# Masks added on VectorE, row factors spread through DRAM, and a new order of pieces in a two-layer trunk

## The chip, the core and the metric

The kernel runs on one core of one Trainium2 chip. TensorE multiplies matrices into eight PSUM banks; VectorE, ScalarE (ACT in the profile) and GpSimd (POOL) do elementwise work; SyncE (SP) and, in places, GpSimd and ScalarE issue the transfers between DRAM and SBUF. The metric is the device time of one execution in microseconds; less is better.

## The reference

Everything is float32. x and mem are 256 rows of 1024, the model has two layers and a last RMS norm:

```python
for layer in range(2):
    h = rms_norm(x, norm_g[layer])
    proj = einsum('btd,dc->btc', h, w_in[layer])          # 1024 x 3584
    sb_q, sb_k, sb_v, sb_g, mb_q, mb_k, mb_v, mb_g, mem_q, mem_g = split(proj)
    o_sb  = stick_breaking_attention(sb_q, sb_k, sb_v) * silu(sb_g)      # 6 heads of 64
    o_mb  = moba_attention(rotary(mb_q), rotary(mb_k), mb_v) * silu(mb_g)  # 6 heads
    m = rms_norm(mem, mem_norm_g[layer])
    mk, mv = split(m @ w_mem_kv[layer])                   # 1024 x 512
    o_mem = memory_attention(mem_q, mk, mv) * silu(mem_g)  # 4 heads
    x = x + concat[o_sb, o_mb, o_mem] @ w_out[layer]      # 1024 x 1024
return rms_norm(x, final_norm_g)
```

Stick-breaking attention is strictly causal: a weight is sigmoid(z) times the product of 1 - sigmoid(z) over the later past positions, computed with logarithms and running sums. With 256 rows and blocks of 256, MoBA is a causal softmax over one block. So both kinds need a triangular mask of -1e30 on the scores of the 128 x 128 blocks on the diagonal, strict for the first, with the diagonal kept for the second. Memory attention has no mask.

## The kernel before

**Precision.** Every weight and every activation that enters a large product is kept as two parts: hi, the value in TensorE's fp32r type, and lo, what is left. A product is three matmuls: hi by hi, hi by lo, lo by hi. The parts of the weights are made on the chip: a cast writes hi (ScalarE or VectorE), a subtraction raw - hi writes lo (VectorE).

**Weights and chunks.** The weights are cut into pieces by group (sb_q, mb_k, ..., wo0 to wo2 for the output projection; the table `ORDER` says in which order each layer takes them), and each piece into chunks of 768 columns by 128 rows, 384 KB. Chunks pass through a ring of 5 raw buffers (`raw`) and 7 pairs hi/lo (`hl`). A raw buffer is loaded again, by SP, right behind the subtraction that read it last. So TensorE needs cast and subtraction of a chunk before it can use it, and VectorE's subtraction also releases the next transfer. A piece is either of the T kind (output transposed, columns on partitions: `hl` is the stationary side; the profile names the moving side first, so its rows read `bank<-T,hl`) or of the N kind (rows on partitions, `bank<-hl,T`). T is the normed activation's transpose in hi and lo.

**The norm of layer 0.** x^T is loaded as 8 row blocks of 128 x 256 into `uT` and scaled by the gains only (`T<-uT,gc`). The factor of each row of x (1/rms) is not known by then: x itself is loaded later (`xs`), its squares are summed on ScalarE, and the factor is multiplied in when a piece leaves PSUM. A piece of the N kind has its rows on partitions and takes the factor as a scalar per partition (`rcx`, `rcm` for mem). A piece of the T kind needs the factors along the free axis, the same on all partitions (`rbx`, `rbm`). For these, `row_stats` (L552 to L575) puts the factors on a diagonal (`dg`, hi and lo, VectorE), multiplies it by a matrix of minus ones on TensorE (`bank<-dg,negone`, float32r, two matmuls for each row block), and copies the result out with the sign turned. In layer 1 the rows are normed before they are transposed, and no factors are needed.

**Scores.** `pair_scores` (L651 to L684) does two heads at a time, in halves of the array (64 of the 128 rows). Behind the products of a pair it adds the mask by 4 bfloat16 matmuls of a mask with the identity, 128 x 128 each, for stick-breaking and MoBA alike. `sb_head` (L686) then has ScalarE read the scores; `soft_head` (L727) takes the maximum of each row with a `TENSOR_REDUCE` (L733) and ScalarE the exponential. The weights of MoBA and of memory attention are transposed in blocks of 32 x 32 on VectorE and turned the rest of the way by a trip through DRAM (`D` to `Z` and back), as are the rotated queries and keys.

**What sets the order.** Nothing is decided while the kernel runs. A planner in the program (class `Sched`) gives every engine its queue: tasks are generators that name the engine they want next and what they need; the planner keeps a clock for each engine from a table of costs, takes the task that can start first, and among those within a slack the one with the smaller priority. Priorities of score, sum and evacuation tasks stand where they are spawned; `_by_form` holds back the half-array products until there are `CROWD` of them, and its table of costs charges for each change between full and half array. Costs, lags, priorities and the loads' places (`X67_AT`, `CST_AT`, `X0_AT`) are constants at the head of the file.

**The start.** Two chunks are issued on ScalarE's queue and the rest on SP's, x^T blocks between them:

```python
load_xT(2, 3); dma_chunk(); load_xT(3, 4); load_xT(4, 6)     # L456 to L459
if j == X67_AT: load_xT(6, 8, now=now)                       # in dma_chunk, L409
```

In the rows, L243 is every matmul (helper `mm`), L259 and L261 ScalarE's copies and activations, L265, L269, L273 and L280 VectorE's forms (tensor by tensor, with scalar, scaling, copy), L346 every transfer of SP, L462 GpSimd's broadcast of a row.

Of the kernel before, what the change touches and what calls it, by code (L numbers as in the profile page):

```python
# [7 lines left out]
F32 = mybir.dt.float32  # L8
# [9 lines left out]
KT = 8  # L18
# [16 lines left out]
P_RX = 1
P_M0 = 12
P_RM = 12
P_M1 = 4
# [168 lines left out]
def hybrid_trunk(ctx: ExitStack, tc: tile.TileContext, x, mem, norm_g, w_in, w_mem_kv, w_out,  # L207
# [26 lines left out]
    def mm(out, lhsT, rhs, start, stop, **kw):  # L234
        n = _free(rhs)
        half = lhsT.shape[0] == 64 or out.shape[0] == 64
        if lhsT.dtype == FR:
            c = max(60.0, n * 0.4167 + 13.0)
# [4 lines left out]
        nc.tensor.matmul(out, lhsT=lhsT, rhs=rhs, start=start, stop=stop, **kw)  # L243
        m = (lhsT.shape[0], out.shape[0])
        S.op("pe", (0.5 * c if half else c) + pe_mode(m, lhsT.dtype))
# [48 lines left out]
    identb = sb("identb", [128, 128], BF)  # L294
    masks = sb("masks", [128, 2, 128], BF)
# [104 lines left out]
    def dma_chunk(now=0.0, q=None):  # L400
# [8 lines left out]
        if j == X67_AT:  # L409
            load_xT(6, 8, now=now)  # L410
# [48 lines left out]
    load_xT(4, 6)  # L459
# [5 lines left out]
    def setup():  # L465
        yield R("pool")
        nc.gpsimd.memset(negone.bitcast(F32), -1.0)
        S.op("pool", 2400.0)
# [3 lines left out]
        nc.gpsimd.tensor_copy(identb, ident)  # L472
        nc.gpsimd.tensor_copy(masks, m.rearrange("p (m c) -> p m c", m=2))
# [78 lines left out]
    def row_stats(l, t, src, key, rc, rb):  # L552
# [667 lines left out]
```

## Time and profile before

| quantity | value |
|---|---|
| time, median of 3 runs | 277.53 us (277.35 to 277.68) |
| the profiled execution | 277.43 us |
| its span | 275.7 us |
| TensorE busy | 268.5 us, 97%, 1709 matmuls |
| VectorE busy | 233.5 us, 85%, 524 instructions |
| ScalarE busy | 182.2 us, 66%, 408 instructions |
| GpSimd busy | 3.8 us, 10 instructions |
| moved by transfers | 62.08 MB, mean 225 GB/s |
| TensorE's granted clock | 0.9 and more in all slices but the last (0.8) |

The profile was taken in one execution; the span is the time between its first and its last record, the rest up to the execution's time lies before and behind. A group in the list of instructions has busy time, mean ns of one, then the idle time of its engine just before, and what ended it. In a piece of timeline, or of the chain of work that ended last, the columns are start, length and what ran; neighbouring instructions of one form stand in one row with their count. The ends of pipelined matmuls are modelled, so that of two rows one behind the other the difference of starts tells the pace, not the length.

### The profile page before, as it was taken

How to read it: one execution, taken by the hardware profiler on the slowest of the kernel's cores; microseconds unless marked ns; L12 is line 12 of the kernel's file. 1: busy time of each engine (PE TensorE's matmuls, PEld its weight loads, DVE VectorE, ACT ScalarE, POOL GpSimd, SP SyncE). 2: the span in 40 equal slices, each digit the busy share in tenths (PEclk: the TensorE clock that was granted, in tenths of full speed). 3: DMA queues.
4: the chain of work that ended last, by engine and by line, in shares of the span. 5: the costliest groups of instructions: out<-in, count | busy, mean ns of one | idle time of the engine just before them, and what ended most of it. 6: DMA issues, size and time to landing. Idle time of an engine off the chain costs nothing.

```text
span 275.7 us, 5015 instructions
## 1 busy us (share of the span) xinstructions
PE 268.5 (97%) x1709; PEld 241.4 (88%) x1709; DVE 233.5 (85%) x524; ACT 182.2 (66%) x408; POOL 3.8 (1%) x10
## 2 busy tenths in 40 slices
PE   8999999999999999999999999999999999999992
PEld 5879999889897898999988899988888898989991
DVE  4879999997999989996889588979889999886172
ACT  3788889995588385873885374549379799543053
POOL 0030000000000000000000000000000000000000
PEclk9999999999999999999999999999999999999998
DMA  6999975778749999873485865795768888580004
GB/s 219 355 394 352 374 249 194 215 218 278 248 134 304 308 289 305 237 256 119 155 267 170 269 185 187 273 300 172 235 216 237 268 214 219 162 269 10 0 0 152
DMA packets 47497, 62.08 MB, mean 225 GB/s; under 512 B 3696, under 2 KB 44016, under 8 KB 47472
## 3 DMA queue, kind: packets, MB, share of 16 engines
q1 hardware_dynamic: 46608, 59.93, 68.7%
q0 software_dynamic: 288, 1.05, 1.1%
q10 hardware_dynamic: 576, 0.79, 0.8%
q8 instruction: 13, 0.21, 0.3%
q14 instruction: 12, 0.10, 0.1%
HBM read 54.67 MB, written 7.08 MB: 224 GB/s over the span
## 4 chain that ended last, share of the span: by engine, by line
PE 93%; DMA 4%; ACT 1%; DVE 1%; SPq 0%; issue 0%; DVEq 0%
PE bank L243 92%; DMA raw<-in_w_in_dram 2%; DMA uT<-xT_dram 1%; PE bank L248 1%; DVE hl L265 0%; ACT hl L259 0%; SPq L346 0%; ACT T L261 0%; ACT ss L261 0%; DVE T L269 0%; ACT junk L261 0%; DVE hl L280 0%; DVE xs L273 0%; DVEq L1216 0%
## 5 line engine op out<-in xcount | busy, mean ns | idle before, releaser
L265 DVE TENSOR_TENSOR hl<-raw,hl 128x768 fp32r<-128x768 f32 (+2 forms) x112 | 101.4, 912 | 11.4 <-ACT hl L259 10.7
L243 PE MATMUL bank<-T,hl 128*128 128x512 f32 (+1 forms) x582 | 106.2, 339 | 0.5 <-DVE hl L265 0.5
L243 PEld LDWEIGHTS bank<-T,hl 128*128 128x128 f32 x582 | 88.9, 189 | 13.8 <-DVE hl L265 0.8
L259 ACT CAST hl<-raw 128x768 fp32r<-128x768 f32 (+2 forms) x99 | 79.0, 811 | 21.1 <-PE bank L243 12.6
L243 PE MATMUL bank<-hl,T 128*128 128x384 f32 (+1 forms) x448 | 81.8, 337 | 0.0
L243 PEld LDWEIGHTS bank<-hl,T 128*128 128x128 f32 x448 | 76.5, 188 | 1.9 <-issue 0.3
L243 PE MATMUL bank<-hl,mxhi 128*128 128x384 f32 (+1 forms) x192 | 45.0, 319 | 0.0
L243 PEld LDWEIGHTS bank<-hl,mxhi 128*128 128x128 f32 x192 | 33.3, 189 | 0.6 <-issue 0.6
L243 PE MATMUL bank<-hl,mxlo 128*128 128x384 f32 (+1 forms) x96 | 30.7, 319 | 0.0
L261 ACT ACTIVATE w<-bank,st 128x256 f32<-128x256 f32 (+1 forms) x40 | 17.3, 451 | 9.0 <-DVE st L733 9.0
L243 PEld LDWEIGHTS bank<-hl,mxlo 128*128 128x128 f32 x96 | 18.1, 189 | 0.5 <-DVE mxlo L265 0.4
L259 ACT COPY gT<-bank 128x256 f32<-128x256 f32 x16 | 5.9, 372 | 18.5 <-PE bank L243 18.3
L261 ACT ACTIVATE junk<-xs 128x384 bf16<-128x384 f32 (+2 forms) x15 | 8.0, 532 | 14.9 <-DVE xs L265 14.2
L261 ACT ACTIVATE ga<-ga 128x768 f32<-128x768 f32 (+1 forms) x24 | 15.1, 631 | 0.7 <-DVE ga L269 0.5
L733 DVE TENSOR_REDUCE st<-bank 128x1 f32<-128x256 f32 (+1 forms) x40 | 12.8, 372 | 1.6 <-PE bank L243 1.6
L261 ACT ACTIVATE T<-uT,gc 128x256 fp32r<-128x256 f32 x24 | 11.4, 502 | 3.6 <-DMA uT<-xT_dram 3.6
L265 DVE TENSOR_TENSOR xs<-bank,xs 128x384 f32<-128x384 f32 (+1 forms) x11 | 5.7, 519 | 8.9 <-PE bank L243 8.9
L763 DVE STREAM_TRANSPOSE D<-w 128x384 f32<-128x384 f32 (+1 forms) x20 | 12.4, 622 | 0.0
L269 DVE SCALAR_TENSOR_TENSOR T<-uT,gc,T 128x256 fp32r<-128x256 f32 x24 | 11.0, 478 | 1.0 <-ACT T L261 1.0
L261 ACT ACTIVATE a<-a 128x384 f32<-128x384 f32 x24 | 11.6, 527 | 0.1
L273 DVE TENSOR_SCALAR w<-w,st 128x256 f32<-128x256 f32 (+1 forms) x40 | 11.1, 327 | 0.0
L265 DVE TENSOR_TENSOR gT<-bank,gT 128x256 f32<-128x256 f32 x16 | 6.7, 419 | 4.3 <-ACT gT L259 3.9
(115 smaller groups left out, 250.1 us busy)
## 6 DMA issues: line engine op xcount, KB each, us to landing
raw<-in_w_in_dram SPq DMA_DIRECT2D x70, 384.0 KB, 4.6
raw<-in_w_out_dram SPq DMA_DIRECT2D x20, 384.0 KB, 4.5
Z<-D SPq DMA_DIRECT2D x10, 384.0 KB, 4.9
raw<-in_w_mem_kv_dram SPq DMA_DIRECT2D x8, 384.0 KB, 3.1
T<-Z SPq DMA_DIRECT2D x24, 96.0 KB, 4.6
uT<-memT_dram SPq DMA_DIRECT2D x8, 256.0 KB, 4.9
Z<-D SPq DMA_DIRECT2D x4, 512.0 KB, 4.3
T<-Z SPq DMA_DIRECT2D x24, 64.0 KB, 3.5
```

The source lines that it names most:

```text
L243: nc.tensor.matmul(out, lhsT=lhsT, rhs=rhs, start=start, stop=stop, **kw)
L248: nc.tensor.transpose(out, in_, idt)
L259: nc.scalar.copy(out, in_)
L261: nc.scalar.activation(out, in_, func, **kw)
L265: nc.vector.tensor_tensor(out, a, b, op=op)
L269: nc.vector.scalar_tensor_tensor(out, a, s, b, op0=op0, op1=op1)
L273: nc.vector.tensor_scalar(out, a, s, None, op0=op)
L733: nc.vector.tensor_reduce(st[:, t:t + 1], sc[:, r0:r1], axis=AX.X, op=OP.max, negate=True)
L763: nc.vector.transpose(o, w[:, :n * 128].rearrange("p (m j r) -> p m j r", j=4, r=32))
```

## The change

1. **Masks.** The matmuls with masks go. A stick-breaking head begins with one VectorE add in place, in PSUM, of a float32 mask to the two diagonal blocks of its scores. For a MoBA head, VectorE's `tensor_tensor_reduce` reads the scores and a mask, writes the negated masked scores to SBUF and keeps their minimum, in place of the `TENSOR_REDUCE`; ScalarE takes the exponential from SBUF with the sign turned, and the score bank is free before that. The mask tiles (`smask`, `cmask`) are float32.
2. **Row factors.** The diagonals and their matmuls go. The factors of 256 rows stand in two columns of a 128 x 32 tile, which VectorE transposes in 32 x 32 blocks (`rt`); GpSimd's queue dumps the 8 rows of 32 to DRAM (two transfers) and, behind them, spreads the row of 256 over all partitions (one transfer). Pieces of the N kind wait for their row block's factors alone and no longer for both.
3. **Start.** x^T blocks 4 to 7 are loaded one at a time, each behind one chunk, and x and the constants one or two chunks later.
4. **Order.** A new `ORDER` of pieces, new orders of the rows within wo pieces (`KORD`), gates computed as 2 + 1 blocks in place of 3 at once, `HALVES` empty (the trips' loads are no longer split in two), new priorities, costs and slacks of the planner.

```diff
-KORD = (0, 1, 2, 3, 4, 5, 6, 7)
+KORD = ((4, 5, 2, 3, 0, 1, 6, 7), (4, 5, 0, 1, 2, 3, 6, 7))
...
-X67_AT = 5
-CST_AT = 9
-X0_AT = 8
-X1_AT = 14
+X_AT = {5: 4, 6: 5, 7: 6, 8: 7}
+CST_AT = 11
+X0_AT = 9
+X1_AT = 15
...
-ORDER = (["sb_qk", "mb_k", "mb_q", "mb_g", "mk", "mv", "mem_q", "sb_v", "sb_g", "mb_v", "mem_g"],
-         ["mk", "mv", "mb_g", "mb_q", "mb_k", "mem_q", "sb_k", "sb_g", "sb_q", "mem_g", "sb_v", "mb_v"])
-GATES = {"sb_g": ((0, 1, 2),), "mb_g": ((0, 1, 2),), "mem_g": ((0,), (1,))}
+ORDER = (["sb_qk", "mb_q", "mb_k", "mk", "mem_q", "mv", "sb_g", "sb_v", "mb_g", "mb_v", "mem_g"],
+         ["mk", "mv", "mb_q", "mb_k", "sb_k", "sb_g", "mem_q", "sb_q", "sb_v", "mb_g", "mb_v", "mem_g"])
+GATES = {"sb_g": ((0, 1), (2,)), "mb_g": ((0, 1), (2,)), "mem_g": ((0,), (1,))}
...
-        if j == X67_AT:
-            load_xT(6, 8, now=now)
+        if j in X_AT:
+            load_xT(X_AT[j], X_AT[j] + 1, now=now)
...
-    load_xT(4, 6)
...
+        nc.gpsimd.tensor_scalar(smask, m[:, 128:256], -1.0, -1.0e30, op0=OP.is_ge, op1=OP.mult)
+        nc.gpsimd.tensor_copy(cmask[:, 128:256], m[:, 128:256])
...
-        yield R("dve", need=["cst"])
-        ts(dg[:, 0, :], ident, rc[:, t:t + 1])
-        yield R("dve")
-        stt(dg[:, 1, :], ident, rc[:, t:t + 1], dg[:, 0, :].bitcast(F32), OP.mult, OP.subtract)
-        _, (pt,) = yield R("pe", alloc=["bank"], need=["setup0"], late=DG_LATE)
-        mm(pt[:, :128], negone, dg[:, 0, :], True, False)
-        mm(pt[:, :128], negone, dg[:, 1, :], False, True)
-        yield R("dve")
-        ts(rb[:, t * 128:(t + 1) * 128], pt[:, :128], -1.0)
...
+    def rows_done(key, name, rb):
+        z = dpool.tile([1, 256], F32, name="rows_" + key)
+        yield R("dve", need=["setup0", (key, "rows", 0), (key, "rows", 1)])
+        nc.vector.transpose(rt, rcx if key == "x" else rcm)
+        S.op("dve", 100.0)
+        yield R("pool")
+        for t in range(2):
+            nc.gpsimd.dma_start(z[:, t * 128:t * 128 + 128].rearrange("o (i a) -> (o i) a", i=4), rt[t:128:32, :])
...
+        yield R("pool", need=[(name, "dump")])
+        nc.gpsimd.dma_start(rb, z.broadcast_to([128, 256]))
...
-        if kind != "mem":
-            yield R("pe")
-            for h in range(2):
-                for j, o in enumerate((slice(0, 128), slice(256, 384))):
-                    if kind == "sb":
-                        mm(sc[h][:, o], masks[:, 0, :], identb, False, j == 1)
-                    else:
-                        mm(sc[h][:, o], identb, masks[:, 1, :], False, j == 1)
...
-        _, (a,) = yield R("act", alloc=["a"], need=[("qkdone", l, "sb", h)])
+        yield R("dve", need=[("qkdone", l, "sb", h)])
         zb = scs.pop((l, "sb", h))
         z = zb[:, :384]
+        zd = zb.rearrange("p (j c) -> p j c", c=256)[:, :, 0:128]
+        tt(zd, zd, smask.unsqueeze(1).broadcast_to([128, 2, 128]), OP.add)
+        _, (a,) = yield R("act", alloc=["a"])
...
+                nc.vector.tensor_tensor_reduce(w[:, r0:r1], sc[:, r0:r1], cmask[:, 256 - r1 + r0:256], -1.0, 3.0e38,
+                                               OP.add, OP.min, st[:, t:t + 1])
...
+            S.free("bank", sc)
+            yield R("act")
+            for t, (r0, r1) in enumerate(reg):
+                act(w[:, r0:r1], w[:, r0:r1], AF.Exp, scale=-1.0, bias=st[:, t:t + 1], accum_out=st[:, 2 + t:3 + t])
```

Three places show what the new order moves. The first is SP's queue at the start: transfers of x^T blocks (`uT`) and weight chunks (`raw`, with the ring's buffer number). Before:

```order
L346 DMA uT_73<-xT_dram 128x256
L346 DMA raw4_93<-in_w_in_dram 128x768
L346 DMA uT_73<-xT_dram 128x256
L346 DMA uT_73<-xT_dram 128x2x256
L346 DMA raw0_89<-in_w_in_dram 128x768
L346 DMA uT_73<-xT_dram 128x2x256
L346 DMA raw1_90<-in_w_in_dram 128x768
```

And now:

```order
L352 DMA uT_73<-xT_dram 128x256
L352 DMA raw4_93<-in_w_in_dram 128x768
L352 DMA uT_73<-xT_dram 128x256
L352 DMA raw0_89<-in_w_in_dram 128x768
L352 DMA uT_73<-xT_dram 128x256
L352 DMA raw1_90<-in_w_in_dram 128x768
L352 DMA uT_73<-xT_dram 128x256
```

The pair of blocks ahead of the chunk in raw0 is gone, the pair behind it is one block, and the others follow behind later chunks.

The second is TensorE's queue at the end of the stick-breaking scores of layer 0, the last products of the third pair of heads and what stands behind (`bank` is a PSUM bank, `T0` the normed x or mem). Before:

```order
L243 MATMUL bank0_101<-sb_q_78,sb_k_80 128x256
L243 MATMUL bank1_102<-sb_q_78,sb_k_80 128x256
L243 MATMUL bank0_101<-sb_q_78,sb_k_80 128x128
L243 MATMUL bank1_102<-sb_q_78,sb_k_80 128x128
L243 LDWEIGHTS masks_68
L243 MATMUL bank3_104<-identb_67,masks_68 128x128
```

And now:

```order
L248 MATMUL bank2_103<-sb_q_78,sb_k_80 128x256
L248 MATMUL bank3_104<-sb_q_78,sb_k_80 128x256
L248 MATMUL bank2_103<-sb_q_78,sb_k_80 128x128
L248 MATMUL bank3_104<-sb_q_78,sb_k_80 128x128
L248 MATMUL bank5_106<-T0_74,hl1_95 128x512
L248 MATMUL bank5_106<-T0_74,hl1_95 128x256
```

Twelve matmuls of the mask stood between the last scores and the next piece; now mem_q's products stand there themselves, in the midst of its first column block.

The third is VectorE's queue in layer 1, where the stick-breaking scores come in. `hl5_99` and `hl6_100` take lo of two chunks, `a0` is the first step of a head behind ScalarE's. Before:

```order
L280 CAST hl1_95<-raw4_93 128x768
L265 TENSOR_TENSOR hl5_99<-raw1_90,hl5_99 128x768
L265 TENSOR_TENSOR gT_85<-bank7_108,gT_85 128x256
L265 TENSOR_TENSOR hl6_100<-raw2_91,hl6_100 128x768
L269 SCALAR_TENSOR_TENSOR a0_109<-bank5_106,a0_109 128x384
L265 TENSOR_TENSOR hl0_94<-raw3_92,hl0_94 128x768
L280 COPY sb_v_82<-bank0_101 128x384
```

And now:

```order
L753 TENSOR_REDUCE st1_139<-bank1_102 128x1
L279 TENSOR_SCALAR w3_115<-w3_115,st6_144 128x256 x2
L271 TENSOR_TENSOR bank6_107<-bank6_107,smask_67 128x2x128
L271 TENSOR_TENSOR bank5_106<-bank5_106,smask_67 128x2x128
L271 TENSOR_TENSOR bank0_101<-bank0_101,smask_67 128x2x128
L271 TENSOR_TENSOR bank3_104<-bank3_104,smask_67 128x2x128
L762 RECIPROCAL st7_145<-st7_145 128x2
L271 TENSOR_TENSOR hl5_99<-raw4_93,hl5_99 128x768
L275 SCALAR_TENSOR_TENSOR sb_q_78<-bank2_103,sb_q_78 128x256
L271 TENSOR_TENSOR hl6_100<-raw0_89,hl6_100 128x768
L275 SCALAR_TENSOR_TENSOR a0_109<-bank6_107,a0_109 128x384
L271 TENSOR_TENSOR hl0_94<-raw1_90,hl0_94 128x768
```

Four adds of the mask stand ahead of the subtractions for two chunks of sb_v; before, nothing that waits for scores stood ahead of these buffers' subtractions.

More of the change, by code (lines that the diff above doesn't have):

```diff
@@ L28 @@
 RAW = 5
-KORD = (0, 1, 2, 3, 4, 5, 6, 7)
+KORD = ((4, 5, 2, 3, 0, 1, 6, 7), (4, 5, 0, 1, 2, 3, 6, 7))
 LAT_SAME, LAT_CROSS = 130.0, 240.0
-PE_LATE = 100.0
-NORM_LATE = 1800.0
-DG_LATE = 400.0
+PE_LATE = 173.4
+NORM_LATE = 1845.2
+DG_LATE = 816.9
+COLD = 3900.0
+PRI = {"sb": (54, 36), "mb": (6, 40), "mem": (44, 48)}
+P_EV = 26
 P_H0 = -8
[L35 to L38, printed above, removed]
+P_RX = 2
+P_M0 = 42
+P_RM = 47
+P_M1 = 50
 URG = 2
-X67_AT = 5
-CST_AT = 9
-X0_AT = 8
-X1_AT = 14
-DMA_GBS = 380.0
+X_AT = {5: 4, 6: 5, 7: 6, 8: 7}
+CST_AT = 11
+X0_AT = 9
+X1_AT = 15
+DMA_GBS = 355.0
 SP_ISSUE = 450.0
+POOL_ISSUE = 1000.0
+POOL_TRIP = 5000.0
 DMA_LAT = 2200.0
@@ L244, in mm @@
         m = (lhsT.shape[0], out.shape[0])
-        S.op("pe", (0.5 * c if half else c) + pe_mode(m, lhsT.dtype))
+        c = (0.5 * c if half else c) + pe_mode(m, lhsT.dtype)
+        S.op("pe", c * (1.8 if S.T["pe"] < COLD else 1.0))
     def tr(out, in_, idt):
@@ L293, in hybrid_trunk @@
     gc = sb("gc", [128, 32])
-    identb = sb("identb", [128, 128], BF)
-    masks = sb("masks", [128, 2, 128], BF)
+    smask = sb("smask", [128, 128])
+    cmask = sb("cmask", [128, 256])
     negT = sb("negT", [128, 128], FR)
@@ L325, in hybrid_trunk @@
     S.res["st"] = Res([sb(f"st{i}", [128, 4]) for i in range(8)])
-    dg = sb("dg", [128, 2, 128], FR)
-    rcx = sb("rcx", [128, 4])
-    rcm = sb("rcm", [128, 4])
+    rcx = sb("rcx", [128, 32])
+    rcm = sb("rcm", [128, 32])
+    rt = sb("rt", [128, 32])
     rbx = sb("rbx", [128, 256])
@@ L340, in queue @@
     def queue(nbytes, run, now):
-        dma_t["t"] = max(dma_t["t"], now) + nbytes / (DMA_GBS if run > 1024 else DMA_GBS_1K)
+        dma_t["t"] = max(dma_t["t"], now) + nbytes / (400.0 if run >= 3072 else DMA_GBS if run > 1024 else DMA_GBS_1K)
         return dma_t["t"] + DMA_LAT
@@ L357, in __init__ @@
             self.nk = CH // width
-            self.kord = KORD if name[:2] == "wo" else tuple(range(KT))
+            self.kord = KORD[layer] if name[:2] == "wo" else tuple(range(KT))
             self.kmap = {}
@@ L466, in setup @@
         yield R("pool")
+        nc.gpsimd.memset(rcx, 0.0)
+        nc.gpsimd.memset(rcm, 0.0)
         nc.gpsimd.memset(negone.bitcast(F32), -1.0)
+        nc.gpsimd.memset(cmask[:, 0:128], 0.0)
         S.op("pool", 2400.0)
@@ L583, in rows_task @@
             yield from row_stats(l, t, src(t), key, rc, rb)
-        S.mark(name)
+        yield from rows_done(key, name, rb)
     def norm_task(l, t, H, done):
@@ L853, in rope_task @@
     def rope_task(l, name, t, acc, scale):
-        _, (rn,) = yield R("act", alloc=["rn"], need=["cst"])
+        _, (rn,) = yield R("act", alloc=["rn"], need=["cst"] if l else ["cst", ("x", "rows", t)])
         n, u = rn
@@ L1115, in main @@
                     yield from N_piece("mv", mT, mneed,
-                                       lambda t, acc: evac_v(l, "mv", t, acc, rcm[:, t:t + 1], 4, "rm"))
+                                       lambda t, acc: evac_v(l, "mv", t, acc, rcm[:, t:t + 1], 4, ("mem", "rows", t)))
                 elif p == "sb_k":
@@ L1119, in main @@
                 elif p in ("sb_v", "mb_v"):
-                    yield from N_piece(p, hT, hneed, lambda t, acc: evac_v(l, p, t, acc, rr_(t), 6, "rx"))
+                    yield from N_piece(p, hT, hneed, lambda t, acc: evac_v(l, p, t, acc, rr_(t), 6, ("x", "rows", t)))
                 elif p == "mem_q":
```

100 lines of the change are left out of this document (53 added, 47 removed).

## The prediction

> **What bounds the kernel now.** I read the busy shares and the chain first, then TensorE's rows in order of time, then the forms of its matmuls. The first row is part 1 of the page; the others are pieces of the chain in order of time (start, length, what).
>
> ```profile
> PE 268.5 (97%) x1709; PEld 241.4 (88%) x1709; DVE 233.5 (85%) x524; ACT 182.2 (66%) x408; POOL 3.8 (1%) x10
> ...
> 6.97 5.83 DMA raw<-in_w_in_dram
> ...
> 14.71 125.85 PE bank L243 x807
> ...
> 149.34 120.90 PE bank L243 x777
> ```
>
> From 14.71 to 270.24 us the chain is nothing but TensorE. One weight chunk holds TensorE up, the one that landed at 12.80; all other casts and transfers are off the path. So a microsecond of TensorE work that goes is a microsecond of time, as long as VectorE (85% busy, and feeding TensorE every chunk) does not fall behind. The span is 275.7; the profiled execution took 277.43, so 1.7 us lie around the span, and its median companion of three runs is 277.53, 0.1 higher: I sum against 277.43 and call the result the median.
>
> **The mask matmuls.** They go, and VectorE gets twelve adds and a new reduce in their place. Rows of TensorE in order of time, then forms (count, busy, mean ns):
>
> ```profile
> 36.12 2.23 PE L243 MATMUL bank<-sb_q,sb_k 64*128 64x256 f32 x24
> 38.29 0.84 PE L243 MATMUL bank<-identb,masks 128*128 128x128 bf16 x12
> 38.94 4.41 PE L243 MATMUL bank<-hl,T 128*128 128x384 f32 x24
> 43.19 0.86 PE L243 MATMUL bank<-T,hl 128*128 128x512 f32 x4
> 43.88 0.34 PE L243 MATMUL bank<-ah,negT 128*128 128x384 f32 x1
> ...
> L243 PE MATMUL bank<-masks,identb 128*128 128x128 bf16 x24 | 1.9, 220 | 0.0
> L243 PE MATMUL bank<-identb,masks 128*128 128x128 bf16 x24 | 1.7, 220 | 0.0
> ```
>
> Matmuls overlap, so the price is start to start: twelve masks take 38.94 - 38.29 = 0.65, 0.054 each; 48 of them are 2.6 us. Nothing hides them: the row behind starts when they end. The single mask in the seeding of the last block is only replaced.
>
> **The row factors.** The diagonals go from VectorE and the eight small matmuls from TensorE:
>
> ```profile
> 20.58 0.34 PE L243 MATMUL bank<-dg,negone 128*128 128x128 f32 x2
> 20.75 2.69 PE L243 MATMUL bank<-T,hl 128*128 128x512 f32 x14
> 23.28 6.95 PE L243 MATMUL bank<-hl,T 128*128 128x384 f32 x39
> ```
>
> Two hold TensorE from 20.58 to 20.75, 0.17 us; there are two for each row block of x and of mem, eight in all: 0.7 us. TensorE loses 3.3 us. It gains two visits to the half-array forms (64 wide on one side; 14 visits in the new order, 12 in the old):
>
> ```profile
> 84.82 1.20 PE L243 MATMUL bank<-T,hl 128*128 128x512 f32 x6
> 85.95 1.52 PE L243 MATMUL bank<-wT,sb_v 128*64 128x256 f32 x16
> 87.41 1.13 PE L243 MATMUL bank<-mem_k,mem_q 64*128 64x256 f32 x8
> 88.47 0.87 PE L243 MATMUL bank<-wT,sb_v 128*64 128x256 f32 x8
> 89.27 7.67 PE L243 MATMUL bank<-T,hl 128*128 128x512 f32 x42
> ```
>
> Six matmuls ahead of a visit take 1.13, where four without one take 0.69 (43.19 to 43.88), so 1.04 for six: 0.09 to enter. Eight alone take 0.80 and sixteen together 1.46: 0.07 to leave, and I put some 0.05 on the first matmul behind. Two visits: +0.4. TensorE's work falls by **2.9 us**; bounds 2.5 (0.4 a visit) and 3.3 (nothing).
>
> **The start.** SP's order there (shown ahead) puts one row block of x^T behind each weight chunk instead of pairs ahead of them. In issue order, the chunk that landed at 12.80 has 5 blocks of 128 KB ahead of it and no longer 8.
>
> ```profile
> 10.00:15.00 5.00, 4.50 (x25) 3.58 (x25) 3.96 (x8) 3.58 (x7) 0.00 (x0) 1.00 1.01 374
> ...
> 9.83 4.37 PE L243 MATMUL bank<-T,hl 128*128 128x512 f32 x23
> 14.71 2.51 PE L243 MATMUL bank<-T,hl 128*128 128x256 f32 x13 [0.50 <-DVE hl L265]
> ```
>
> The engines were full (1.01 busy, 374 GB/s, the last two columns), so 393 KB less is 1.05 us earlier. TensorE lost there 0.50 of idle time and about 0.5 that the modelled ends cover (23 matmuls stand between 9.83 and 14.71, where pairs take 0.345: 4.0 of 4.9). I take **-0.9**; bounds 0 (the next chunk becomes the late one) and -1.0. The x rows for the statistics come one chunk later; ACT waits for them in its queue, but the casts behind have over a microsecond in hand.
>
> **VectorE.** Forms and one burst (start, length), then its idle:
>
> ```profile
> L733 DVE TENSOR_REDUCE st<-bank 128x1 f32<-128x256 f32 x28 | 10.5, 412 | 1.0 <-PE bank L243 1.0
> L733 DVE TENSOR_REDUCE st<-bank 128x1 f32<-128x128 f32 x12 | 3.0, 278 | 0.6 <-PE bank L243 0.6
> L265 DVE TENSOR_TENSOR gT<-bank,gT 128x256 f32<-128x256 f32 x16 | 6.7, 419 | 4.3 <-ACT gT L259 3.9
> L541 DVE TENSOR_SCALAR ss<-ss 128x1 f32<-128x1 f32 x12 | 2.0, 167 | 0.1
> L269 DVE SCALAR_TENSOR_TENSOR mv<-bank,rcm,mv 128x256 f32<-128x256 f32 x4 | 1.8, 480 | 0.2 <-ACT mv L261 0.2
> L280 DVE CAST hl<-raw 128x768 fp32r<-128x768 f32 x10 | 5.5, 548 | 0.0
> ...
> 184.67 2.41 DVE L733 TENSOR_REDUCE st<-bank 128x1 f32<-128x256 f32 x7 [0.96 <-PE bank L243]
> 187.00 0.15 DVE L742 RECIPROCAL st<-st 128x2 f32<-128x2 f32 x1
> ```
>
> Back to back, seven reduces of 412 take 187.00 - 184.67 = 2.33, 0.33 each: the pace is the mean less 0.08. Twelve mask adds are like gT (256 wide, one operand in PSUM): 0.34 each, 4.1 us. The masking reduce appears in no row. It is 24 main instructions and, by the order, 24 one-element ones behind them. Below, a reduce (0.26 on average of the two widths) and the pace of a one-element instruction, 0.08: 0.35 a pair; above, the slowest two-tensor form from PSUM (480 for 256, 0.33 for 128) and 0.17 unoverlapped: 0.57. A gain is excluded, since the reduce alone was there before. I take 0.35, the pace at which nearly all forms of VectorE run. That adds 2.0, the adds 4.1 and the split gates about 1.2; nine wide casts go to ACT (-4.2), diagonals and their copies go (-3). VectorE's total stays within a microsecond; ACT takes on some 13 us and is at 66%. So only places count, and one is tight.
>
> It is the one shown ahead: in layer 1 the adds for the stick-breaking scores stand on VectorE's queue **ahead of the subtractions of two sb_v chunks** (hl_99, hl_100), and wait for TensorE's scores. Behind the scores TensorE does 4 short matmuls (0.69) and 12 of 384 wide at 4.25/24 = 0.177, so it needs hl_99 2.8 us after the scores and hl_100 3.9 after. VectorE: 0.3 to notice, two adds 0.67, a reciprocal 0.07, a subtraction 0.87: 1.9; then 0.34 + 0.87: 3.1. Slack 0.9 and 0.8. But VectorE must have arrived: from the first MoBA scores to these adds it has, counted in the new order at these paces, 12 pairs (4.2), 4 reduces 1.2, 10 scalings 2.4, 4 transposes 1.9, 2 subtractions 1.7, rest 1.3: 12.7 us. TensorE between the same points does 50 matmuls of T and hl (8.6) and six pairs of scores (4.2): 12.8. It arrives just in time, so a part of the slack will be lost to waits that sums don't have. I put **+1.0** on stalls of TensorE here and at the first adds in layer 0 (bounds 0 and 2.7: 0.22 more for each of 12 pairs).
>
> **The trips of the row factors.** rbx, once a copy out of PSUM, now makes two hops through DRAM on GpSimd's queue; six products on VectorE wait for it, with all its chunks queued behind them. Rows: ACT's factor, GpSimd's issue, transfers to landing (KB, median us).
>
> ```profile
> 29.18 0.18 ACT L261 ACTIVATE rcx<-rcx 128x1 f32<-128x1 f32 x1
> ...
> 61.90 0.73 POOL L462 DMA_DIRECT2D gb<-in_norm_g_dram  x1 [42.02 <-DMA ga<-Z]
> ...
> uT<-xT_dram SPq DMA_DIRECT2D x4, 128.0 KB, 3.9
> gb<-in_norm_g_dram POOLq DMA_DIRECT2D x1, 512.0 KB, 6.6
> gc<-gcols_dram SPq DMA_DIRECT2D x1, 16.0 KB, 1.9
> ```
>
> In the new order the scores stand behind four pieces of 24 (17.0), 32 matmuls of mk (5.5) and 8 more (1.4), from 23.28 - 1.1: at 46.1. The products need 2.3, so rbx must be there by 43.8. The factor is ready at about 31 (x one chunk later). The trip: three issues of 0.73, 1.9 for the tiny dump and 3.9 for the 128 KB of the spread: 8.0, landing at 39: hidden, price nothing. By the upper row (6.6 twice) it is 15.4, landing at 46.4: VectorE and then TensorE 2.6 late. Below, 1.9 twice: 6.0. GpSimd has nothing else to do there, and the second factors (rbm) have far longer.
>
> [...]
>
> **Sum.** 277.43 - 2.9 - 0.9 + 1.0 = 274.6; I say **274.7**, its own range 273.4 to 275.9.
>
> **Rivals.** (1) The masking reduce costs its upper row: +2.6 on top at the tight place, 277.3, no change to be told. For it: VectorE's 85% and no row of the form. Against: every form of VectorE seen here runs at one element per tick. (2) The trips come late by the upper row: 277.3, or 275.5 to 277 between the rows. (3) **Slower**: the masking reduce goes over its scores twice, 0.70 a pair. The 12 pairs of layer 1 then delay the adds, and with them the sb_v chunks and every chunk of the ring behind them, by 4.2: 278.9. It decides from 0.63 a pair, where the whole gain is used up; slack in layer 0 is larger (its chunks are needed over 3 us after the burst), so it counts once. For it: the order makes these adds a gate between TensorE and its weights that was not there. (4) TensorE's saving turns into waits at the adds entirely: 277.4.
>
> **Chances.** Forecast 0.66; (1) 0.10; (2) 0.08, half of it faster; (3) 0.13; (4) 0.03. A difference under 0.2% (0.55 us) can't be told from none here. Faster 0.70, same 0.17, slower 0.13. The range leaves out (3) and the low edge of the forecast: 273.4 to 277.8.
>
> **What would show it.** TensorE's busy time near 265, with no rows of masks or dg; the first idle at 13 to 15 us gone. Masking reduces of 280 and 410 ns with a short row behind; if they take 600 and more, (3). VectorE's products with rbx at 42 to 44 without idle time ahead from a DMA; else (2). TensorE's idle or stretched starts at 200 to 215 us: a microsecond. I am wrong if TensorE's gaps elsewhere, where chunks have 2 us and more in hand, are larger than here.

## The result, and the profile after

The changed kernel takes **276.08 us** (median of 6 runs, 275.43 to 277.10) against 277.61 for the kernel before on the same chip (6 runs): a ratio of **0.9948**, 95% interval 0.9927 to 0.9970. It is faster by half a per cent, half of what was forecast (274.7, one per cent), and above the forecast's own range (273.4 to 275.9). Here and below, medians are of all runs, and ratios leave out the few that lie over 1.5% above the fastest of their kernel.

The profiled execution is the longest of the six, 277.10 us, with a span of 275.2; 1.0 us of what follows is therefore not in the median. First the page's busy times and the chain by engine.

```profile
PE 265.4 (96%) x1653; PEld 239.1 (87%) x1653; DVE 229.6 (83%) x543; ACT 193.0 (70%) x441; POOL 7.6 (3%) x19
...
PE 84%; DVE 9%; DMA 2%; issue 1%; ACT 1%; DVEq 0%
```

TensorE is busy 3.1 us less than before, and the span is only 0.5 shorter: TensorE waits now. Before, the chain was TensorE from 14.71 us on; now 9% of it is VectorE. Where TensorE stands still, its timeline shows (start, length, what; in brackets the idle time ahead and what ended it):

```profile
38.97 7.16 PE L248 MATMUL bank<-T,hl 128*128 128x512 f32 x40
48.49 2.23 PE L248 MATMUL bank<-sb_q,sb_k 64*128 64x256 f32 x24 [2.37 <-DVE sb_k L275]
...
65.81 2.24 PE L248 MATMUL bank<-uT 64*128 64x128 f32 x24
68.61 1.31 PE L248 MATMUL bank<-T,hl 128*128 128x512 f32 x6 [0.56 <-DVE st L740]
...
263.13 0.34 PE L248 MATMUL bank<-hl,mxhi 128*128 128x384 f32 x1
263.78 0.28 PE L248 MATMUL bank<-junk 128*128 128x256 bf16 x1 [0.32 <-ACT junk L267]
```

Three places: 2.4 us ahead of the stick-breaking scores of layer 0, 0.6 behind the MoBA scores of layer 0, and 0.5 (263.13 to 263.78 where a matmul of this kind takes 0.17) ahead of the matmul that seeds the last block. The stall at 13 to 15 us is gone. At 200 to 215 us in layer 1, the place that the forecast called tight, there is none.

The first of the three, seen from VectorE (above) and ScalarE (below the dots):

```profile
45.80 0.96 DVE L271 TENSOR_TENSOR hl<-raw,hl 128x768 fp32r<-128x768 f32 x1 [2.61 <-ACT hl L265]
46.68 0.42 DVE L275 SCALAR_TENSOR_TENSOR mem_k<-bank,mem_k 128x256 f32<-128x256 f32 x1
47.02 1.09 DVE L275 SCALAR_TENSOR_TENSOR sb_q<-sb_q,rbx 128x256 f32<-128x256 f32 x3
48.02 1.09 DVE L275 SCALAR_TENSOR_TENSOR sb_k<-sb_k,rbx 128x256 f32<-128x256 f32 x3
...
44.94 0.84 ACT L265 CAST hl<-raw 128x768 fp32r<-128x768 f32 x1 [4.18 <-DMA raw<-in_w_mem_kv_dram]
```

VectorE idles 2.6 us, and not for the products with rbx (47.02): it idles at the lo subtraction that stands ahead of them in its queue. That subtraction waits for ScalarE's cast, and the cast for a chunk of `w_mem_kv` that was issued at 38.34 and landed at 44.92. By SP's order it is the first chunk of mv, which TensorE uses from 54.97 on. Both queues stand behind a chunk that nobody needs for another ten microseconds, and the products that TensorE does need stand behind it.

How full the transfer engines were is in the windows (last two columns: busy share of the transfer engines, GB/s), the kernel before first, the changed one behind the dots:

```profile
35.00:40.00 5.00, 5.00 (x49) 4.50 (x49) 4.66 (x15) 4.26 (x9) 0.00 (x0) 1.00 0.64 216
40.00:45.00 5.00, 5.00 (x33) 4.92 (x31) 5.00 (x13) 4.75 (x14) 0.00 (x0) 1.00 0.53 200
45.00:50.00 5.00, 5.00 (x31) 4.40 (x30) 5.00 (x13) 4.48 (x10) 0.00 (x0) 1.00 0.71 213
...
35.00:40.00 5.00, 5.00 (x30) 4.88 (x29) 5.00 (x13) 5.00 (x11) 0.58 (x1) 1.00 0.76 238
40.00:45.00 5.00, 5.00 (x31) 4.38 (x30) 3.09 (x8) 0.82 (x4) 0.00 (x0) 1.00 0.93 275
45.00:50.00 5.00, 2.63 (x25) 2.13 (x25) 4.20 (x11) 4.45 (x9) 0.00 (x0) 1.00 0.89 322
```

Between 40 and 50 us the engines are 0.9 busy where they were 0.5 to 0.7.

What TensorE gained and lost in the profiled execution, by kinds of matmul (sums of the differences between neighbouring starts; a stall is what such a difference has over the usual one of its form):

| term | us |
|---|---|
| mask matmuls | -2.6 |
| matmuls of the diagonals | -0.7 |
| changes between full and half array, without stalls | +0.6 |
| stalls up to 15 us (0.9 before, 0.2 now) | -0.7 |
| stalls in layer 0 (2.41 and 0.64) | +3.05 |
| stall at the seeding | +0.5 |
| the rest, in steps under 0.1 | -0.5 |
| first to last start of TensorE, 268.76 to 268.34 | -0.4 |

### The profile page after: what moved, and what is told of

Its sections match the earlier page's. It is cut to its first block, busy times and chain, and to the rows that moved or that the text cites. A ratio compares the mean times of both kernels' runs of the same rounds, so it can differ in the third digit from the quotient of the medians.

```text
span 275.2 us, 4955 instructions
## 1 busy us (share of the span) xinstructions
PE 265.4 (96%) x1653; PEld 239.1 (87%) x1653; DVE 229.6 (83%) x543; ACT 193.0 (70%) x441; POOL 7.6 (3%) x19
## 4 chain that ended last, share of the span: by engine, by line
PE 84%; DVE 9%; DMA 2%; issue 1%; ACT 1%; DVEq 0%
PE bank L248 84%; DVE hl L271 3%; DMA raw<-in_w_mem_kv_dram 2%; DVE al L271 1%; DVE bank L271 1%; PE bank L254 1%; DVE xs L271 1%; DVE mem_q L275 0%; ACT junk L267 0%; ACT hl L265 0%; DVE a L275 0%; DVE ah L286 0%; DVE sb_k L275 0%; DVE sb_q L275 0%; DVE mv L275 0%
## 5 line engine op out<-in xcount | busy, mean ns | idle before, releaser
L271 DVE TENSOR_TENSOR hl<-raw,hl 128x768 fp32r<-128x768 f32 (+3 forms) x114 | 101.4, 899 | 11.7 <-ACT hl L265 10.5
L265 ACT CAST hl<-raw 128x768 fp32r<-128x768 f32 (+2 forms) x111 | 87.4, 796 | 15.2 <-PE bank L248 4.4
L248 PE MATMUL bank<-hl,T 128*128 128x384 f32 (+1 forms) x448 | 80.3, 336 | 0.0
L267 ACT ACTIVATE ga<-ga 128x256 f32<-128x256 f32 (+1 forms) x36 | 17.4, 488 | 0.9 <-DVE ga L275 0.7
L267 ACT ACTIVATE a<-a 128x384 f32<-128x384 f32 x24 | 12.4, 533 | 0.0
L267 ACT ACTIVATE w<-w,st 128x128 f32<-128x128 f32 (+1 forms) x24 | 10.6, 446 | 0.7 <-DVE st L740 0.5
L267 ACT ACTIVATE w<-bank,st 128x256 f32<-128x256 f32 x16 | 7.4, 474 | 2.4 <-DVE st L753 2.4
```

The costliest lines, as they stand in the source:

```text
L265: nc.scalar.copy(out, in_)
L267: nc.scalar.activation(out, in_, func, **kw)
L271: nc.vector.tensor_tensor(out, a, b, op=op)
```

## The experiments

The stalls given for each run are from its profiled execution and made as in the table above. The changed kernel's runs spread (275.3 to 278.3 and once 280.2; the kernel before, 276.7 to 279.6 in 119 runs), and the 95% intervals of the ratios (given in brackets) reach 0.2 to 0.35% to each side, some 0.7 us, so the stalls say more than the medians. But each stall is of one execution.

### The changed kernel again

> The changed kernel as it is, as the base of the other three and to see how much its stalls vary. All theories: 276.1, between 275.4 and 277.1. In the first profile of it TensorE stood still 2.4 us ahead of the stick-breaking scores of layer 0 (45.84 to 48.49), 0.6 behind the MoBA scores (67.67 to 68.61) and 0.5 ahead of the seeding of the last block (263.13 to 263.78); the theory that the first of these hangs on transfers on a full set of queues expects its size to differ from execution to execution, by 0.5 us and more, and the other two to be there again.

276.49 us (275.32 to 280.18, 12 runs), ratio 0.9962 (0.9938 to 0.9986). Stalls: 0.62 at 9 us, 1.81 ahead of the scores, 0.64 behind the MoBA scores, 0.48 at the seeding. The last two are the same to 0.01 us; the first of layer 0 moves, as transfers do.

### The seeding matmul

```diff
+    seedz = sb("seedz", [128, 256], BF)          # set to zero on GpSimd at the start
-    mm(accs[2, 1][:, :256], junk[:, :128], junk[:, :256], True, True)
+    mm(accs[2, 1][:, :256], seedz[:, :128], seedz, True, True)
```

> The seeding matmul of the last block reads a zero tile of its own in place of junk, which ScalarE overwrites with squares. Theory: it waited for ScalarE's last square into junk, so the 0.5 us ahead of it goes and the time falls by 0.4 to 0.5 against the changed kernel. Rival: the wait moves to the copy that seeds the block, or to the end of the statistics, and the time is the same within 0.2.

276.07 us (0.9949, 0.9927 to 0.9971), and 276.19 (0.9965, 0.9943 to 0.9986) when run again. No stall at the seeding in either. That the time falls by as much is not shown: the unchanged kernel's two ratios were 0.9948 and 0.9962. But the mechanism is: the change took `junk` as operand in place of the mask tile that no longer exists, and `junk` is where ScalarE dumps its squares.

### Without the trip, without most of mem's rows

```diff
-            nc.gpsimd.dma_start(z[...], rt[t:128:32, :])     # x only; also the spread of rbx
+            # rbx is set to one on GpSimd at the start
```

> Leaves out the trip of the factors of x through DRAM (two dumps and the spread of 128 KB): rbx is set to one on GpSimd at the start, so the T pieces of layer 0 are not multiplied by their rows' factors. Theory one, that the last chunk of mk (landed at 44.9) holds VectorE in front of the products with rbx: no change beyond 0.4 us, the stall ahead of the scores stays above 1.5. Theory two, that the trip (31.5 to about 43.9) holds them: 1.5 to 2.5 us faster, the stall is gone.

275.62 us (0.9926, 0.9907 to 0.9945). Stall ahead of the scores 0.23, behind the MoBA scores 0.72, at the seeding 0.48. Neither theory had this. The products stand behind the same subtraction as before and come right behind it; but the chunk's cast began at 43.00 and no longer at 43.8 to 44.9. So in this execution the gain is not that rbx needn't be waited for: the chunk itself came earlier, with the trip's transfers gone.

```diff
-        (q or nc.sync).dma_start(dst, src)
+        if name and name[0] == "mem":
+            nc.sync.dma_start(dst[:, :128], src[:, :128])    # 128 of 1024 columns
```

> Loads only the first 128 of the 1024 columns of mem for its row statistics (the rest of the buffer is set to one), which takes 0.9 MB off the transfer queues between 26 and 45 us, with every instruction in its place. Theory one (mk's chunks are late because the transfer engines are full there): mk's last chunk lands 1 to 2 us earlier and the time falls by 1 to 2 us. Theory two (the trip): the chunk lands earlier as well, but the products wait for rbx at 43 and later, and the time falls by 1 at most. Theory three (VectorE itself is late with its work there): no change.

275.33 us (0.9927, 0.9905 to 0.9949). The cast began at 42.89, the stall ahead of the scores is 0.72. 0.9 MB less on the queues is worth 0.8 to 1.2 us against the changed kernel's two medians: late transfers are the immediate cause of most of this stall.

### The products ahead of the chunk

Three instructions of VectorE change places, with the seeding mended. The list is VectorE's order, shortened; the reload of the chunk's buffer on SP's queue moves back with the subtraction:

```diff
 TENSOR_TENSOR rn / STREAM_TRANSPOSE D
-TENSOR_TENSOR hl<-raw,hl 128x768        (mv's first chunk)
-SCALAR_TENSOR_TENSOR mem_k<-bank,mem_k
 SCALAR_TENSOR_TENSOR sb_q<-sb_q,rbx x3
 SCALAR_TENSOR_TENSOR sb_k<-sb_k,rbx x3
+TENSOR_TENSOR hl<-raw,hl 128x768
+SCALAR_TENSOR_TENSOR mem_k<-bank,mem_k
```

> Three instructions of VectorE in layer 0 change places, nothing else: the lo subtraction of mv's first chunk (and the reload of its buffer) and mk's first evacuation go behind the six products with rbx, that is behind and no longer ahead of what the stick-breaking scores wait for; the seeding matmul reads its own zero tile as before. Theory one (head of the line: rbx landed at 40 to 44, but the products stand behind mv's chunk, which landed at 43.8 to 44.9 and which TensorE needs only at 55): the stall of 1.2 to 2.4 us ahead of the scores falls below 0.5, VectorE does 2 us of its work in what was idle time, the 0.6 us behind the MoBA scores shrinks as well, and the time falls to 274.5 to 275.3. Theory two (the trip of the factors is late itself): VectorE idles for rbx instead, and the time stays at 275.5 to 276.1. Theory three (VectorE's total work in layer 0): the stall comes back at the MoBA scores and the time is 275.5 and more.

276.57 us (0.9947, 0.9922 to 0.9972): nothing gained, and none of the three theories came out whole. The trace says why. TensorE's timeline, then ScalarE's:

```profile
46.06 2.23 PE L250 MATMUL bank<-sb_q,sb_k 64*128 64x256 f32 x24
48.22 4.47 PE L250 MATMUL bank<-T,hl 128*128 128x512 f32 x24
53.88 2.74 PE L250 MATMUL bank<-hl,T 128*128 128x512 f32 x14 [1.19 <-DVE mem_q L277]
...
47.34 0.63 ACT L269 ACTIVATE junk<-gb 128x512 bf16<-128x512 f32 x1 [0.35 <-DMA gb<-in_mem_dram]
```

The scores come without a stall, since rbx was there (the products ran at 43.87). But 6 us later the first piece of mv waits 1.2 us for a PSUM bank, behind mem_q's evacuation, behind ScalarE's steps of the stick-breaking heads, behind the squares of mem's second row block, whose load was issued at 40.16 and landed at 47.32. The stall moved from one late transfer to the next.

> The version with the products ahead of mv's chunk, and of mem's rows only 128 of 1024 columns loaded for the statistics (0.9 MB less). Theory one (late transfers are the whole of the stalls between 45 and 55): no stall above 0.3 us is left there, and the time is 274.0 to 274.9, the forecast. Theory two (VectorE's own work): 0.6 us and more of stalls stay between 45 and 70, and the time is 275.0 to 275.8.

The same with 0.9 MB of mem's rows left out: **274.98 us** (0.9912, 0.9889 to 0.9934). No stall is left between 6 and 65 us, as theory one had it; behind the MoBA scores 0.72 stay, as theory two had it, so late transfers are not the whole. With the queue in order and the transfers light, the forecast is nearly reached.

For a version that keeps the whole computation, the second row block of mem goes to a buffer of its own (an unused half of the gates' tile) and is issued earlier, with and without the swap:

```diff
+    gb2 = gT[:, 4:8, :].rearrange("p k c -> p (k c)")
+        if p.name == "mem_q" and p.layer == 0 and kk[-1] == KT - 1:
+            nc.sync.dma_start(gb2, mem_r[:, 1, :])
```

> Only the second row block of mem loaded early, the products in their old place. Theory one: mv's first chunk, issued just behind this load, lands later by its 0.5 MB (up to 1.4 us), so the stall ahead of the scores grows to 2 to 3 us, and the time is 276.2 to 277.5. Theory two (bandwidth doesn't matter): as the version with the own zero tile, 275.6 to 276.2.

> The version with the products ahead of mv's chunk, and the second row block of mem loaded into a buffer of its own (the unused half of the gates' tile) and issued some 3 us earlier, ahead of the dump of the turned queries, where the transfer engines were 0.6 to 0.8 busy (35 to 40 us). With the products moved alone, the stall had gone from the scores (45.8) to the pieces of mv (52.3, 1.4 us), at the end of a chain that began with this load (issued 40.16, landed 47.32). Theory one (a chain of late transfers on full queues): with both moved the stalls between 45 and 55 add up to under 0.7 us and the time is 274.5 to 275.3. Theory two (VectorE and ScalarE are late with their own work there): the stall shows up somewhere else between 45 and 70, and the time stays at 275.8 to 276.8.

Without the swap 280.13 us (1.0089, 1.0055 to 1.0123): 0.5 MB ahead of mv's chunk moved its cast from about 44.5 to 48, and the stall ahead of the scores grew to 4.57. That is more than was expected (theory one, 276.2 to 277.5) and the clearest sign that transfers set this stretch; part of it is the lower clock (0.66 from 50 to 55 us) told of in the last section. With the swap 277.07 us (0.9981, 0.9952 to 1.0011), a stall of 1.79 at 52.3: nothing gained either. The loads can be shuffled there, but something that is waited for comes late.

### VectorE's added work

```diff
-        tt(zd, zd, smask.unsqueeze(1).broadcast_to([128, 2, 128]), OP.add)
+        if l:
+            tt(zd, zd, smask.unsqueeze(1).broadcast_to([128, 2, 128]), OP.add)
```

> The changed kernel without the six mask adds of the stick-breaking heads in layer 0 (their scores stay unmasked), 2.0 us of VectorE's work between 50 and 53 us. Theory: TensorE's 0.6 us behind the MoBA scores (it waits for a bank that VectorE's masking reduces free) comes from VectorE's queue being full from 45 to 68, so it goes, and the time falls by 0.4 to 0.7 us. Rival: it comes from the place of the reduces alone, behind ScalarE's work; the stall stays above 0.4 and the time the same within 0.3.

276.80 us (0.9973, 0.9945 to 1.0000); stalls 1.76 ahead of the scores, 0.50 behind the MoBA scores. The rival holds: 2 us of VectorE's work less moved neither. What the 0.6 us is remains open; it was between 0.4 and 0.7 in every run with the changed kernel's order of pieces, except with the row factors the old way (below), where it is gone, and TensorE waits there for a bank that the masking reduce frees.

### The start, and the masks alone

The first is the changed kernel with x^T issued as before, every other instruction in its place:

```diff
+    nc.sync.dma_start(uT[:, 4:6, :], xT_r[:, 4:6, :])        # behind load_xT(3, 4)
-            load_xT(X_AT[j], X_AT[j] + 1, now=now)
+            if j == 5:
+                nc.sync.dma_start(uT[:, 6:8, :], xT_r[:, 6:8, :])
```

> The changed kernel with x^T blocks 4 to 7 issued as before (pairs ahead of the chunks), all other instructions in their places. By the prediction's term the chunk that landed at 12.80 comes late again, TensorE stands still 0.7 to 1.0 us at 13 to 15, and the time rises by 0.5 to 0.9. Rival: the late start is absorbed by the stall ahead of the scores in layer 0, which is set by transfers and VectorE and not by TensorE: no change beyond 0.3.

277.24 us (0.9991, 0.9966 to 1.0017), 0.8 to 1.2 above the changed kernel's medians, where each of the two ratios is good to some 0.7 us. TensorE's stall at 13.5 is back (0.72). The stall ahead of the scores (1.89) is as large as in the changed kernel (2.41 and 1.81), so it did not absorb the late start; the one behind the MoBA scores is 0.4 in place of 0.64.

The second is the kernel before without its mask matmuls (scores unmasked):

```diff
-                    mm(sc[h][:, o], masks[:, 0, :], identb, False, j == 1)
-                    mm(sc[h][:, o], identb, masks[:, 1, :], False, j == 1)
```

> The kernel before without its 48 mask matmuls (scores unmasked), every other instruction in its place. By the prediction's term TensorE's work falls by 2.6 us and the time with it, 277.6 to about 275.0, since no other engine stands in the way. Rival: VectorE and the chunks were nearly late already, so part of the 2.6 comes back as waits and the time falls by 1.5 at most.

275.06 us (0.9906, 0.9879 to 0.9932), 2.58 less than the 277.64 of the kernel before beside it. The term was 2.6.

### Other orders of layer 0

```diff
-["sb_qk", "mb_q", "mb_k", "mk", "mem_q", "mv", "sb_g", "sb_v", "mb_g", "mb_v", "mem_g"]
+["sb_qk", "mb_k", "mb_q", "mb_g", "mk", "mv", "mem_q", "sb_v", "sb_g", "mb_v", "mem_g"]
```

> The changed kernel (with the zero tile for the seeding matmul) and the order of layer 0's pieces as before: mb_g stands between mb_q and mk again. If the new order makes the transfers late: no stall above 0.5 us between 40 and 60, and the time falls from 276.1 to 274.0 to 275.2, the forecast without its last 0.5. If the trips and VectorE's added work make them late: the stalls stay at 1.2 us and more, and the time is 275.6 to 276.8.

> The same with another order of layer 0, mk two pieces later: sb_qk, mb_q, mb_k, sb_g, mem_q, mk, mv, sb_v, mb_g, mb_v, mem_g. If mem's early need is the cause: stalls between 40 and 60 under 0.5 us, time 274.0 to 275.2. Rival (the trips and VectorE): 275.6 to 276.8.

> The same with mem_q ahead of mk and sb_g ahead of mv: sb_qk, mb_q, mb_k, mem_q, mk, sb_g, mv, sb_v, mb_g, mb_v, mem_g. If mem's early need is the cause: stalls smaller than with the changed kernel's order (mk 5.6 us later, mv 8.5 us), 274.3 to 275.5. Rival: 275.6 to 276.8.

> The changed kernel with the zero tile for the seeding matmul, once more, as the base of the other three: 276.1, 275.3 to 277.5, with 1.2 to 1.9 us of stall ahead of the scores of layer 0 and 0.6 to 0.7 behind the MoBA scores.

280.03 us (1.0051, 1.0020 to 1.0082), 277.60 (1.0014) and 278.66 (1.0004); the base 276.19. Stalls ahead of the scores: 1.41, 2.50 and 0.35 (base 1.44). None of the three is faster than the base, and no range of times that was expected, the theory's or the rival's, was met. The theory that mem is wanted one piece too early **falls** for the first two: with the order of before the stall is as large. In the third it did shrink to 0.35, but others came: 0.6 in the MoBA scores (65.5) and 1.4 at 107.2, where TensorE waits for the values mb_v from ScalarE. The first has such stalls too, 0.9 at 108.2 and some 0.5 each at 85.9 and 125.2. These two also spread most of all (277.0 to 282.6 and 275.9 to 282.6), and their profiled executions are not their slowest; what the slow ones wait for is open. In the first, ahead of the scores, VectorE idled at the subtraction of another chunk:

```profile
43.87 0.69 DVE L271 TENSOR_TENSOR hl<-raw,hl 128x512 fp32r<-128x512 f32 x1 [1.39 <-ACT hl L265]
...
46.37 1.08 DVE L275 SCALAR_TENSOR_TENSOR sb_q<-sb_q,rbx 128x256 f32<-128x256 f32 x3
```

In every one of these orders the products stand at 45.5 to 46.8 us, behind whatever is late there. In the kernel before, they ran at 33.46 and the scores at 36.12.

### Row factors the old way

The diagonals and their matmuls are put back, the rest of the change stays (seeding mended; six of the planner's constants set so that its plan suits this).

```diff
+        ts(dg[:, 0, :], ident, rc[:, t:t + 1])
+        stt(dg[:, 1, :], ident, rc[:, t:t + 1], dg[:, 0, :].bitcast(F32), OP.mult, OP.subtract)
+        mm(pt[:, :128], negone, dg[:, 0, :], True, False)
+        mm(pt[:, :128], negone, dg[:, 1, :], False, True)
+        ts(rb[:, t * 128:(t + 1) * 128], pt[:, :128], -1.0)
-        nc.vector.transpose(rt, rcx if key == "x" else rcm)
-        (the two dumps and the spread)
...
+P_RX = 12, DG_LATE = 400, CST_AT = 10, X0_AT = 8, X1_AT = 14, P_M0 = 12
```

> The changed kernel (with the zero tile for the seeding matmul) with the row factors as in the kernel before: diagonals on VectorE, eight small matmuls on TensorE, no trips; the planner's constants for the loads of x and the constants and two priorities set so that its plan suits that. The scores then stand some 10 us earlier in TensorE's order. If the trips are the root: no stall above 0.5 us ahead of the scores, eight matmuls more (0.7 us), and the time is 274.6 to 275.6 (276.1 - 1.4 + 0.7 - 0.3 or so). If late transfers stop TensorE whatever stands there: stalls of 1 us and more turn up elsewhere between 30 and 70 us, and the time is 276.3 to 277.5.

> The same with a slightly different plan (the constants loaded two chunks later, the matmuls of the diagonals placed later). Same expectations: 274.6 to 275.6 if the trips are the root, 276.3 to 277.5 if not; should only one of the two be fast, the place of single transfers decides and not the trips.

**275.36 us** (0.9927, 0.9902 to 0.9953) and 275.56 (0.9931, 0.9906 to 0.9957), both medians below the changed kernel's and with runs close together (274.5 to 276.4). By time alone the difference to the changed kernel with the seeding mended, 0.5 to 0.8 us, is within the intervals; the traces carry more. The first one's chain, its scores on TensorE, and (behind the last dots) ScalarE in the second one:

```profile
1.19 137.97 PE bank L248 x852
...
148.30 119.00 PE bank L248 x751
...
33.09 5.44 PE L248 MATMUL bank<-hl,T 128*128 128x384 f32 x30
38.46 2.23 PE L248 MATMUL bank<-sb_q,sb_k 64*128 64x256 f32 x24
...
48.07 0.84 ACT L265 CAST hl<-raw 128x768 fp32r<-128x768 f32 x1 [1.38 <-DMA raw<-in_w_mem_kv_dram]
```

In the first plan the chain is TensorE from 1.19 to 267.3 us, without a break; no stall above 0.15 us is left after 6 us, the one behind the MoBA scores and the one at 13 us included. The scores stand at 38.46, 10 us earlier than in the changed kernel. In the second plan a chunk of `w_mem_kv` still comes late (the last row), VectorE idles 1.27 us behind it, and TensorE loses some 0.7 us at 49 to 50; but the scores have long been done. So the root lies with the trips: they cost TensorE nothing directly and save it 0.7 us, and by the time that they take they push the products and the scores into the stretch where chunks and mem's rows are late. Since some constants of the plan differ too (x is loaded one chunk earlier, priorities are others), this is shown for these two plans; no run keeps the trips with the new constants, so the two are not told apart.

## Why the prediction was wrong, and which terms held

**The mask matmuls (-2.6): right.** 2.6 in the trace, 2.58 when they alone are taken out. **The diagonals (-0.7): right**, 0.74 in the kernel before. **Two visits more (+0.4):** 0.6. **The start (-0.9):** 0.7 in the profiled execution, 0.8 to 1.2 when undone (each to some 0.7 us).

**The masking reduce (0.35 a pair, bounds 0.35 and 0.57): cheaper than the lower bound.** Its forms, with the reduce of memory attention and the mask add beside them:

```profile
L753 DVE TENSOR_REDUCE st<-bank 128x1 f32<-128x256 f32 x16 | 6.4, 413 | 0.0
L740 DVE CUSTOM_DVE_ANT_0 w<-bank,cmask 128x256 f32<-128x256 f32 x12 | 4.8, 416 | 0.0
L271 DVE TENSOR_TENSOR bank<-bank,smask 128x256 f32<-128x256 f32 x12 | 4.3, 427 | 0.1
L740 DVE CUSTOM_DVE_ANT_0 w<-bank,cmask 128x128 f32<-128x128 f32 x12 | 3.0, 284 | 0.0
L740 DVE DVE_READ_ACCUMULATOR2_ANT st<- 128x1 f32 x24 | 2.0, 84 | 0.0
```

It takes what a plain reduce takes, and the short read of the minimum hides under the next main instruction: in the layer-1 rows below mains follow each other at 0.34. Rivals 1 (0.57 a pair) and 3 (0.70, slower) needed the opposite and fall. (By rival 1's own sum the gain is used up at 0.58 a pair, not at the 0.63 of rival 3.) The mask adds cost the 0.34 of the sum. The argument that every form of VectorE seen there runs at one element per tick doesn't hold for a row shown beside it: the reduce took 412 ns for 256 elements and 278 for 128, 1.05 ns for each element more, but the cast of 768 took 548 ns in all. VectorE's total, put within a microsecond, fell by 3.9.

**The stalls of TensorE (+1.0, at the adds of layer 1 and the first adds of layer 0): the step that failed.** They were looked for behind the adds, and layer 0 was taken to have more slack than layer 1. The place that was singled out as tight cost nothing. TensorE, then VectorE there:

```profile
202.44 1.47 PE L248 MATMUL bank<-sb_q,sb_k 64*128 64x256 f32 x16
203.84 0.97 PE L248 MATMUL bank<-T,hl 128*128 128x512 f32 x4
204.65 5.56 PE L248 MATMUL bank<-hl,T 128*128 128x384 f32 x31
...
201.53 0.42 DVE L740 CUSTOM_DVE_ANT_0 w<-bank,cmask 128x256 f32<-128x256 f32 x1
201.87 0.42 DVE L753 TENSOR_REDUCE st<-bank 128x1 f32<-128x256 f32 x1
203.29 1.43 DVE L271 TENSOR_TENSOR bank<-bank,smask 128x256 f32<-128x256 f32 x4
```

VectorE reaches the adds as the scores end, and TensorE goes on without a gap through the two chunks whose subtractions stand behind the adds. The slack of 0.8 to 0.9 was enough. The stalls came ahead of scores, not behind adds, and in layer 0: what the prediction gave as its sign of being wrong.

**The trips (hidden, price nothing): the other step that failed,** and the costlier. The trip took longer than the 8.0 of the sum, as GpSimd's queue and the landing of the two dumps and the spread show (least, middle and most of the three; the spread's is the most). The last row is of the kernel before, VectorE's first products with rbx:

```profile
31.96 1.33 POOL L583 DMA_DIRECT2D rows_x<-rt  x2 [9.44 <-DVE rt L579]
37.79 0.58 POOL L587 DMA_DIRECT2D rbx<-rows_x  x1 [4.49 <-DMA rows_x<-rt]
...
DMA to landing us min/median/max: 4.5/5.0/6.1
...
33.46 1.09 DVE L269 SCALAR_TENSOR_TENSOR sb_q<-sb_q,rbx 128x256 f32<-128x256 f32 x3
```

31.66 (end of the turn) to 43.9, 12.2 us: the tiny dumps took 4.5 and 5.0 in place of 1.9, issued on transfer engines that were 1.08 busy (32 to 35 us), and the spread 6.1 in place of 3.9, on engines 0.89 busy (37.8 to 43.9). The issues themselves took 0.58 us twice and 0.75 once, where the row before had 0.73. The spread landed as the deadline of 43.8 came; in five other profiled executions of this order it landed at 40.3, 42.9, 43.7, 43.9 and 45.9. In all six the products came later still, behind the chunk, so the landing stopped nothing, but it had next to nothing in hand. What failed was the question. I asked when rbx must be there, and took 46.1 for the start of the scores (TensorE did stand ready then) as a gain without a price, with "all its chunks queued behind them". Not asked was what stands **ahead** of the products in VectorE's queue once they have moved 13 us back: the subtraction of a chunk, behind a cast, behind a transfer that is late on full engines. Rival 2 named the right part of the change, by the wrong arrival; that its time (275.5 to 277) holds the measured one is luck.

**The seeding ("only replaced"):** the operand that replaced the mask is written by ScalarE just then: 0.48 us.

So the terms of work came to -2.7 and the start to -0.7, near the forecast (-2.9 and -0.9); the stalls came to 2.3 to 3.8 us in six profiled executions of this order (seeding included or already mended), in place of 1.0, and but for the seeding they are in layer 0.

## What to carry to other kernels

When a step is moved later because its data will come later, read what stands ahead of it in the queue at its new place and what that waits for, not only whether its own data will be there. A transfer of half a kilobyte need not be short when the transfer engines are full (4.5 and 5.0 us here, with the engines 1.08 busy; the same dumps for mem, at 62 us with the engines 0.54 busy, took 1.6 and 3.4), and an operand that is "only a dummy" carries the dependences of whatever else writes it. Where the next late item stands close behind, as here, moving one shows the next: test with the load taken away before building the repair.

## What the runs showed of the hardware

Behind some stalls TensorE ran at a lower granted clock, so that the stall cost more than itself. In the kernel before, no execution of 119 had a mean granted clock below 0.994; nor had any of the 12 with the row factors the old way. Kernels that stall had some: in the mended changed kernel 4 executions of 24 had 0.990 and took 277.7 to 278.4 us, the others 275.3 to 277.8 with a median of 276.1. The windows of two such executions, the one with x^T issued as before and (behind the dots) the one with mem's second row block early, have the granted clock in the third column from the end:

```profile
45.00:50.00 5.00, 3.15 (x23) 2.50 (x24) 4.21 (x11) 4.37 (x9) 0.00 (x0) 0.94 0.94 335
50.00:55.00 5.00, 5.00 (x29) 4.21 (x26) 4.57 (x11) 3.82 (x11) 0.54 (x1) 0.71 0.86 231
...
45.00:50.00 5.00, 1.96 (x12) 1.46 (x10) 1.19 (x2) 2.06 (x4) 0.00 (x0) 1.00 0.91 325
50.00:55.00 5.00, 3.51 (x24) 3.06 (x24) 4.59 (x14) 4.15 (x12) 0.00 (x0) 0.66 0.77 217
```

After stalls of 1.9 and 4.6 us the clock is below full while TensorE is busy again. By these columns 1.75 us of full clock is missing in the first (0.06 x 5 + 0.29 x 5) and 1.70 in the second (0.34 x 5), and the 24 score matmuls of the second took 3.65 us instead of the changed kernel's 2.23. The length of the stall alone doesn't tell: behind 1.9 us in one execution the clock was lower, behind 2.4 in another (the first profile of the changed kernel) it stayed at 1.00. What lowers it is not shown. Still, the lower clock is part of why the kernels with stalls spread more between executions; not all of it, since with layer 0's order of before 281.15 us came at a mean clock of 0.996 and 282.60 at 0.994.
